# Two output-gate blocks moved from the attention's filler into the gate stage, and the second value tiles computed in another order

## The chip, the cores and the metric

The kernel runs on one core of one Trainium2 chip. The metric is the device time of one execution in microseconds; lower is better. The program is one launch that reads float32 inputs from DRAM and writes a float32 output of 1024 x 1024.

## The reference

One streaming-encoder block on 16 meta tokens and 1024 tokens of width 1024. What matters here is the mixer:

```python
u = rmsnorm(h, norm_mix)
a, q, k, v, r, lr, ga, gb = split(u @ w_in)             # widths 512, 256, 256, 512, 512, 16, 1024, 1024
y_a = (mix(multiscale_pool(a)) * pool_scale) @ w_pool_out
o   = gla_chunked(q, k, v, log_sigmoid(lr @ w_gate_up + b_gate) / 16)     # 4 heads, chunks of 64 tokens
y_b = (rmsnorm(o, gla_norm) * silu(r)) @ w_gla_out
m   = sigmoid(ga) * y_a + sigmoid(gb) * y_b
h   = h + m @ w_out
```

A squared-ReLU feed-forward layer (1024 to 4096 to 1024) and a last norm follow. The change concerns 256 of the 1024 columns of `gb`, which are blocks 6 and 7 of 128 columns, and the order in which one half of `v` is computed.

## The kernel before

All large products run on TensorE as three products each: every operand is split into a high part (rounded by ScalarE, `act.activation(hi, raw, ACT.Copy)`) and a low part (the rest, by VectorE or GpSimd), and high times high, high times low and low times high are summed in PSUM (`mm3`, L245 to L251). A "product" below is one such matmul of 128 x 128 weights on 512 columns, unless another width is given. Tokens lie in two halves of 512; meta tokens stand ahead of half 0. The normed input sits in SBUF as `th` and `tl` (high and low, one pair for each half).

The stages follow each other:

1. **Start** (L690): norm, transposes, the first half of `v`.
2. **Gate stage** (`Quarters` L286, `gate_result` L891, `gate_stage` L932): blocks of 128 output columns of `w_in` are computed in pairs. For a pair and the two token halves, the 2 x 2 product over two halves of the inner dimension is formed from seven quarter products (P1 to P7) instead of eight. Each quarter product is 4 inner tiles of 128 x three matmuls of 512 columns, so a pair costs 7 x 12 = 84 products, where the plain way (`project`, L447) costs 2 blocks x 2 halves x 8 tiles x 3 = 96. `BLOCKS` (L616) lists 20 blocks, so ten pairs: `ga` 0 to 7, `q`, `r`, and `gb` 0 to 5. Results go to DRAM (`ga_dram`, `q_dram`, `r_dram`, `gb_dram`).
3. **Pooling** and the first block of `k`.
4. **Attention** (`gla`, L1524): four units (pair of heads, token half) in the order (0,0), (1,0), (0,1), (1,1). Of each unit, `inside` (decays and scores, L1359) runs beside `across` (states and output, L1445) of the unit before. These are chains of small steps that pass between engines, and TensorE would wait in them. So work called filler is poured between the steps: `fill` (L1276) is a list of independent projections, and after each step `pour` takes as many products from it as cover the latency that the step states in its `yield`. The order of TensorE's instructions is therefore written out when the program is built, and it is fixed. Filler, in order: second block of `k`; second half of `v` (`v_second`); the last two blocks of `gb` the plain way (`gb_pair(6)`); `y_a` (`ya_block`, 4 x 48 products); `y_b` of half 0 (`yb_block(j, 0)`, 4 x 24 products). What is left after the last unit runs behind it.
5. `y_b` of half 1, out projection, feed-forward, last norm. `early_gates` (L1202) fixes the recorded order on ScalarE and VectorE from the last `across` on.

Steps of the last `across` by line: L1402 and L1403 make the decayed keys `mix` (`kl`) and queries; L1456 transposes the keys on TensorE and L1457 copies them to SBUF; L1464 multiplies keys by values into PSUM tile `b_m` (bank `m2`, of which there is one, L1126); seven steps at L1470 run the state from chunk to chunk on VectorE; L1479 and L1489 make the output in the same bank, with a one-column read by ScalarE between them (L1484); L1498 squares, L1501 sums, L224 to L233 take the inverse root, L1503 scales, L1507 transposes, L1514 and L1516 multiply by the silu gate, L1518 rounds to `yg` and L1521 takes the low part. `y_b` of half 1 reads that `yg`.

Steps of one output of the filler: `ya_block` multiplies by the gate at L1058 (VectorE) and stores to `ma_dram`; `yb_block` of half 0 multiplies by the `gb` gate at L1257 and adds `ma` at L1262 (both VectorE), stores the sum (ScalarE's DMA queue, L1265), rounds it at L1268 (ScalarE) and takes the low part in two pieces at L1272 (GpSimd).

`pooled_back` (L1147) loads the pooled operand (four DMAs of 1 MB, GpSimd's queue) over `th` and `tl` of half 1, once nothing else reads those; `ya_block` needs it. `gate_load` (L1036) loads one `ga` gate tile.

## Time and profile before

| | us |
|---|---|
| median of 3 runs | 1192.87 (1192.79 to 1193.24) |
| the profiled execution | 1193.63 |
| its span, first to last instruction | 1191.9 |
| gate stage, steady part | about 43 to 237 |
| pooling, first `k` | about 237 to 302 |
| attention with filler | about 302 to 463 |
| `y_b` of half 1, out projection, feed-forward | about 463 to 1184 |
| VectorE, ScalarE busy | 895.5 (75%), 643.5 (54%) |
| DMA mean rate | 167 GB/s |

Stage borders are read from the times at which the lines of each stage run in the trace. Times of rows below are microseconds from the start of the span. A matmul's busy time overlaps the next one, so its price is the distance between starts. Waits are put down to what ended last.

### The profile page before, as it was taken

What the parts mean: (1) busy time and instruction counts of PE and PEld (TensorE: products, weight loads), DVE (VectorE), ACT (ScalarE), POOL (GpSimd) and SP (SyncE); (2) the same over time, 40 slices, a digit from 0 to 9 for tenths busy, and PEclk for the clock granted to TensorE, in tenths of its full rate; (3) what the DMA queues carried; (4) which work ended last, traced back from release to release, by engine and by line L of the source; (5) the groups of instructions that cost most, each with busy time, mean ns of one, the idle gap of its engine ahead of it and who ended that gap; (6) DMA issues with size and microseconds to landing.
All of it is one profiled execution on the core that took longest, in us unless ns stands there. A gap on an engine that the chain in (4) does not pass through costs nothing.

```text
span 1191.9 us, 18477 instructions
## 1 busy us (share of the span) xinstructions
PE 1177.9 (99%) x6762; PEld 985.7 (83%) x6762; DVE 895.5 (75%) x1436; ACT 643.5 (54%) x1172; POOL 76.1 (6%) x122
## 2 busy tenths in 40 slices
PE   8999999999999999999999999999999999999997
PEld 8888888898998887788888888888888888888885
DVE  7886577657667887998996677767665887787695
ACT  7767567754546432548754554545554444445454
POOL 2200010000103226010000000000000000000000
PEclk9999999999999999999999999999999999999999
DMA  8247784435206677993264444445399963333532
GB/s 261 37 115 178 220 193 126 150 111 156 72 20 242 193 250 253 329 247 131 91 201 146 165 151 141 159 137 181 125 310 321 335 193 95 99 95 97 168 98 89
DMA packets 149515, 199.03 MB, mean 167 GB/s; under 512 B 10712, under 2 KB 81136, under 8 KB 148624
## 3 DMA queue, kind: packets, MB, share of 16 engines
q1 hardware_dynamic: 142992, 179.69, 47.3%
q0 software_dynamic: 5120, 15.80, 5.8%
q10 hardware_dynamic: 1312, 2.36, 0.5%
q8 instruction: 53, 0.87, 0.3%
q14 instruction: 38, 0.31, 0.1%
HBM read 138.04 MB, written 68.16 MB: 173 GB/s over the span
## 4 chain that ended last, share of the span: by engine, by line
PE 92%; DVE 3%; DMA 3%; ACT 1%; issue 1%; POOL 0%; SPq 0%; ACTq 0%; DVEq 0%
PE b_mm L249 10%; PE b_mm L251 10%; PE b_mm L250 10%; PE b_ms L250 10%; PE b_ms L249 10%; PE b_ms L251 10%; PE b_x L250 8%; PE b_x L249 8%; PE b_x L251 8%; PE b_sc L1356 1%; PE b_mx L249 1%; PE b_mx L251 1%; PE b_mx L250 1%; DMA t<-gb_dram 1%; PE b_ms L1848 1%
## 5 line engine op out<-in xcount | busy, mean ns | idle before, releaser
L249 PE MATMUL b_mm<-th,w1h 128*128 128x512 f32 (+1 forms) x308 | 115.4, 375 | 0.8 <-DVE acc L1952 0.5
L251 PE MATMUL b_mm<-th,w1l 128*128 128x512 f32 (+1 forms) x308 | 114.2, 371 | 0.0
L250 PE MATMUL b_mm<-tl,w1h 128*128 128x512 f32 (+1 forms) x308 | 114.1, 371 | 0.0
L250 PE MATMUL b_x<-tl,w1h 128*128 128x512 f32 (+1 forms) x264 | 100.1, 379 | 0.0
L249 PE MATMUL b_x<-th,w1h 128*128 128x512 f32 (+1 forms) x264 | 100.1, 379 | 0.0
L251 PE MATMUL b_x<-th,w1l 128*128 128x512 f32 (+1 forms) x264 | 99.7, 378 | 0.0
L267 ACT ACTIVATE w1h<-raw 128x512 fp32r<-128x512 f32 x98 | 60.7, 620 | 25.2 <-PE b_ms L250 12.7
L268 DVE TENSOR_TENSOR w1l<-raw,w1h 128x512 fp32r<-128x512 f32 x98 | 67.0, 684 | 8.6 <-ACT w1h L267 8.6
L267 ACT ACTIVATE w1h<-fs 128x512 fp32r<-128x512 f32 x78 | 48.8, 628 | 43.6 <-PE b_ms L250 26.3
L249 PEld LDWEIGHTS b_mm<-th,w1h 128*128 128x128 f32 x308 | 57.8, 188 | 11.7 <-issue 1.6
L251 PEld LDWEIGHTS b_mm<-th,w1l 128*128 128x128 f32 x308 | 57.8, 188 | 10.1
L250 PEld LDWEIGHTS b_mm<-tl,w1h 128*128 128x128 f32 x308 | 57.9, 188 | 9.6
L268 DVE TENSOR_TENSOR w1l<-fs,w1h 128x512 fp32r<-128x512 f32 x78 | 53.3, 685 | 14.0 <-ACT w1h L267 13.8
L267 ACT ACTIVATE w1h<-bt 128x512 fp32r<-128x512 f32 x44 | 27.8, 632 | 66.6 <-issue 62.2
L251 PEld LDWEIGHTS b_x<-th,w1l 128*128 128x128 f32 x264 | 49.7, 188 | 9.5
L249 PEld LDWEIGHTS b_x<-th,w1h 128*128 128x128 f32 x264 | 49.6, 188 | 9.5
L250 PEld LDWEIGHTS b_x<-tl,w1h 128*128 128x128 f32 x264 | 49.6, 188 | 9.3
L2020 DVE TENSOR_TENSOR bt<-w,w 128x512 f32<-128x512 f32 x80 | 54.6, 683 | 0.0
L267 ACT ACTIVATE fxh<-bt 128x512 fp32r<-128x512 f32 x36 | 22.8, 632 | 56.3 <-issue 50.7
L1955 ACT ACTIVATE acc<-acc 128x512 f32<-128x512 f32 x48 | 30.3, 631 | 37.8 <-DVE acc L1952 37.8
L268 DVE TENSOR_TENSOR w1l<-rawx,w1h 128x512 fp32r<-128x512 f32 x44 | 30.1, 686 | 23.2 <-ACT w1h L267 23.2
L268 DVE TENSOR_TENSOR w1l<-bt,w1h 128x512 fp32r<-128x512 f32 x44 | 30.4, 690 | 20.9 <-ACT w1h L267 20.9
(537 smaller groups left out, 3411.5 us busy)
## 6 DMA issues: line engine op xcount, KB each, us to landing
hf_dram<-acc SPq DMA_DIRECT2D x112, 256.0 KB, 2.1
raw<-hf_dram SPq DMA_DIRECT2D x112, 256.0 KB, 2.6
w<-in_w_ff_dram SPq DMA_DIRECT2D x64, 256.0 KB, 4.5
raw<-in_w_in_dram SPq DMA_DIRECT2D x22, 512.0 KB, 4.7
raw<-in_w_ff_dram SPq DMA_DIRECT2D x16, 512.0 KB, 4.2
rawx<-in_w_ff_dram SPq DMA_DIRECT2D x16, 512.0 KB, 4.2
wt_dram<-in_w_out_dram POOLq DMA_DIRECT2D x6, 1024.0 KB, 10.6
rawx<-in_w_in_dram SPq DMA_DIRECT2D x10, 512.0 KB, 4.3
```

What stands on the lines that cost most here:

```text
L249: pe.matmul(ps, ah, bh, start=first and i == 0, stop=False, skip_group_check=more)
L250: pe.matmul(ps, ah, bl, start=False, stop=False, skip_group_check=more)
L251: pe.matmul(ps, al, bh, start=False, stop=last and i == n - 1, skip_group_check=more)
L267: act.activation(hi, a, ACT.Copy)
L268: low = lambda: dve.tensor_tensor(lo, a, f32(hi), ALU.subtract)
L1356: pe.matmul(b[to, e, j], kk[r, s], qq[r, s], start=True, stop=True, tile_position=(e * CH, u * CH))
L1848: pe.transpose(b[j][:, i], u[:, (4 * j + i) * P : (4 * j + i + 1) * P], ident)
L1955: act.activation(h[w], h[w] if u is not None else b, ACT.Relu)
L2020: dve.tensor_tensor(bt, w, S["w2"][q[3:]][:, i], ALU.add if q[2] == "+" else ALU.subtract)
```

## The change

`BLOCKS` gets `gb` blocks 6 and 7, so the gate stage computes eleven pairs. `gb_pair` and its `gb_block` are gone, and the filler with them is 96 products shorter; that also takes two weight blocks out of the filler's weight ring. `v_second` computes the tiles of token half 1 first, then the meta tile, calls `pooled_back` and `gate_load` twice (as `gb_pair` did), then the tiles of half 0. Lines behind `gb_block` stand 21 lower in the new file (L1262 is L1241), those behind the list of filler 22 lower (L1456 is L1434).

```diff
-        + [("r", h, C_R + h * P) for h in range(HEADS)] + [("gb", d, C_GB + d * P) for d in range(6)]
+        + [("r", h, C_R + h * P) for h in range(HEADS)] + [("gb", d, C_GB + d * P) for d in range(8)]
...
     def v_second():
-        for t in range(9):
+        for t in (4, 5, 6, 7, 8, 0, 1, 2, 3):
             rows, leave = v_tile(1, t, by_k=True)
             for k in range(0, KT, 2):
                 rows(k, 2)
                 yield 6 * 256 / 2400
             leave()
+            if t == 8:
+                pooled_back()
+                gate_load()
+                gate_load()
...
-    def gb_pair(d):
-        def fn(*wbs):
-            for half, at, n in MAIN[::-1]:
-                for u in range(2):
-                    yield from gb_block(d + u, [(half, at, n)], False)(wbs[u])
-                    if u and half:
-                        pooled_back()
-                    elif not half:
-                        yield "one"
-            gate_load()
-            gate_load()
-        return fn
...
-    step(fill, gb_pair(6), W1, [w_cols(C_GB + d * P) for d in (6, 7)])
```

**TensorE, the last `across`.** Before, between the output's first part (L1479) and its second (L1489), half 0 of `y_b` (`yg` is its operand, L249 to L251):

```order
L1479 MATMUL b_m_4729<-v_2711,scc 64x128 x16
L249 MATMUL b_mx<-yg_3510,w1h 128x512
L250 MATMUL b_mx<-yg_3510,w1h 128x512
L251 MATMUL b_mx<-yg_3510,w1l 128x512
L249 MATMUL b_mx<-yg_3510,w1h 128x512
L250 MATMUL b_mx<-yg_3510,w1h 128x512
L251 MATMUL b_mx<-yg_3510,w1l 128x512
L1489 MATMUL b_m_4729<-W,mix 64x128 x4
L1489 MATMUL b_m_4729<-S,mix 64x128 x2
L1489 MATMUL b_m_4729<-W,mix 64x128 x10
```

In the whole last `across`, 12 products of `y_b` stand ahead of the key transposes, 9 behind them, then 21, 6, 30 and 18 in the places that follow. Now (the first row is the last product of `y_b` of half 0, the last row is the first of half 1):

```order
L251 MATMUL b_mx<-yg_3655,w1l 128x512
L1434 MATMUL b_ms<-ident,mix 128x128 x4
L1442 MATMUL b_m_4808<-v_2850,mix 64x128 x16
L1457 MATMUL b_m_4832<-v_2850,scc 64x128 x16
L1467 MATMUL b_m_4832<-W,mix 64x128 x4
L1467 MATMUL b_m_4832<-S,mix 64x128 x2
L1467 MATMUL b_m_4832<-W,mix 64x128 x10
L1485 MATMUL b_m_4877<-ident,mix 128x128 x8
L249 MATMUL b_mm<-yg_3651,w1h 128x512
```

The filler ends ahead of the last `across`, and its six steps follow each other with nothing between them. Up to that place the number of products between two attention steps is the same in both programs; only their kind differs, `y_a` standing where `gb` stood and `y_b` of half 0 where `y_a` stood.

**VectorE, `inside` of the last unit beside `across` of the one before**, up to the sum of squares (TENSOR_REDUCE). Before, with the gate product of `y_a` (L1058) between the attention's steps:

```order
L1389 TENSOR_TENSOR n_2868<-n_2864,ends 128x16x2x16
L1391 TENSOR_TENSOR f<-n_2864,ends 128x16x32
L1419 COPY_PREDICATED scc<-mask,b_sc 128x512
L1058 TENSOR_TENSOR o<-b_mm,t_2715 128x512
L1419 COPY_PREDICATED scc<-mask,b_sc 128x512
L1389 TENSOR_TENSOR kq_2255<-n_2868,ends 128x8x2x32
L1391 TENSOR_TENSOR f<-n_2868,ends 128x8x64
L1058 TENSOR_TENSOR o<-b_mm,t_2715 128x512
L1501 TENSOR_REDUCE small<-mix 128x8
```

Now, with the two steps of a `y_b` output (L1236 is L1257, L1241 is L1262):

```order
L1367 TENSOR_TENSOR n_3007<-n_3003,ends 128x16x2x16
L1369 TENSOR_TENSOR f<-n_3003,ends 128x16x32
L1397 COPY_PREDICATED scc<-mask,b_sc 128x512
L1236 TENSOR_TENSOR t_2854<-b_mm,t_2854 128x512
L1397 COPY_PREDICATED scc<-mask,b_sc 128x512
L1241 TENSOR_TENSOR t_2854<-t_2854,o 128x512
L1367 TENSOR_TENSOR kq_2394<-n_3007,ends 128x8x2x32
L1369 TENSOR_TENSOR f<-n_3007,ends 128x8x64
L1236 TENSOR_TENSOR t_2854<-b_mx,t_2854 128x512
L1241 TENSOR_TENSOR t_2854<-t_2854,o 128x512
L1479 TENSOR_REDUCE small<-mix 128x8
```

Each output of filler in this unit now has two VectorE steps where it had one.

## Prediction

> **What bounds the kernel now.** I read the page first, then TensorE's waits, then stretches of the three stages that the change touches.

> ```profile
> span 1191.9 us, 18477 instructions
> PE 1177.9 (99%) x6762; PEld 985.7 (83%) x6762; DVE 895.5 (75%) x1436; ACT 643.5 (54%) x1172; POOL 76.1 (6%) x122
> PE b_m L1489 <- ACT small L1484: 1.3, 1, 1.3
> PE b_mx L249 <- DVE t L1257: 0.2, 1, 0.2
> 100.00:200.00 100.00, 100.00 (x438) 82.06 (x437) 67.72 (x106) 63.16 (x112) 7.44 (x14) 1.00 0.72 182
> 331.50:336.50 5.00, 5.00 (x44) 5.00 (x43) 2.70 (x10) 4.68 (x12) 0.46 (x1) 1.00 0.01 3
> 402.00:438.00 36.00, 36.00 (x456) 29.78 (x453) 30.56 (x57) 14.17 (x24) 7.73 (x8) 1.00 0.71 223
> ```

> TensorE (PE) is busy for 99% of the span, and its list of waits is short: the two rows above are the only ones inside the attention. Busy time alone proves little for pipelined matmuls, but the distance between starts does: in 100 us of the gate stage (columns: length, then busy time and count of PE, weight load, VectorE, ScalarE, GpSimd, then clock, DMA share, GB/s) there are 438 products, 0.228 us each, with VectorE 68% and ScalarE 63% busy. In the attention (402 to 438) PE never stops either. So the program is bound by the number of TensorE products, as long as filler covers the attention's chains. That condition is what the change touches: 12 products fewer in all, but 84 more in a stage that has no gaps and 96 fewer in one that needs them as cover.

> **The change part by part.**

> *Gate stage.* One more pair is 84 products x 0.228 = **+19.2 us**. The other engines' shares above are per pair, so they stay below one; two more weight blocks and four stores per pair lie within a DMA share of 0.72. Nothing else is on the path.

> *Filler up to the last `across`.* Between any two attention steps stand as many products as before, so PE's clock time there is unchanged as long as no step comes late: **0** in itself.

> *Order of the value tiles.* The same 216 products of 256 columns. `pooled_back` now goes out behind the meta tile, and 96 products of the half-0 tiles stand between it and the first `y_a`; 44 of them take 5.0 us in the second window above, so they cover 11 us, the attention's steps apart.

> ```profile
> tl<-pm_dram POOLq DMA_DIRECT2D x2, 1024.0 KB, 8.7
> ```

> The first half of that operand must land by then: 8.7 us is hidden, the second half is wanted one output (12 products, 2.7 us) later. If the cover failed, it would cost the 1 or 2 us by which a load is later. I take **0**. GpSimd's two weight blocks for `gb` (four pieces each) leave its queue, and `pooled_back` stands behind one of them less, so nothing there is later.

> *The last `across`.* Here the cover is gone. Before, from the start of `y_b` (438.45) to the start of the second half-1 block (470.00) PE runs 31.5 us, 108 products among them. Now PE reaches the same place with no half-0 product left, and the chain runs bare. Its steps, one engine at a time:

> ```profile
> 437.12 0.69 DVE L1516 TENSOR_TENSOR mix<-b_m,mix 128x512 f32<-128x512 f32 x1 [2.23 <-PE b_m L1507]
> 437.85 1.29 ACT L1518 ACTIVATE yg<-mix 128x512 fp32r<-128x512 f32 x2 [0.28 <-DVE mix L1516]
> 438.45 0.40 PE L249 MATMUL b_mx<-yg,w1h 128*128 128x512 f32 x1
> 439.12 0.42 DVE L1402 TENSOR_TENSOR mix<-kq,ends 128x256 f32<-128x256 f32 x1
> 439.45 0.69 DVE L1521 TENSOR_TENSOR yg<-mix,yg 128x512 fp32r<-128x512 f32 x1
> 440.39 0.74 DVE L1419 COPY_PREDICATED scc<-mask,b_sc 128x512 f32<-128x512 uint8 x1
> 440.51 1.06 ACT L1601 ACTIVATE wx<-raw 128x1024 fp32r<-128x1024 f32 x1
> 441.21 0.60 PE L1456 MATMUL b_ms<-ident,mix 128*128 128x128 f32 x4
> 441.62 0.68 DVE L1257 TENSOR_TENSOR t<-b_mx,t 128x512 f32<-128x512 f32 x1
> 441.84 0.60 ACT L1457 ACTIVATE mix<-b_ms 128x512 f32<-128x512 f32 x1 [0.27 <-PE b_ms L1456]
> 442.33 0.69 DVE L1262 TENSOR_TENSOR t<-t,o 128x512 f32<-128x512 f32 x1
> 443.80 1.10 PE L1464 MATMUL b_m<-v,mix 64*64 64x128 f32 x32
> 444.97 0.35 DVE L1470 SCALAR_TENSOR_TENSOR W<-S,ends,b_m 128x128 f32<-128x128 f32 x1 [1.95 <-PE b_m L1464]
> 445.36 2.27 DVE L1470 SCALAR_TENSOR_TENSOR W<-W,ends,b_m 128x128 f32<-128x128 f32 x6
> 449.86 1.10 PE L1479 MATMUL b_m<-v,scc 64*64 64x128 f32 x32
> 453.66 0.15 ACT L1484 ACTIVATE small<-b_m 128x2 f32<-128x2 f32 x1
> 455.10 1.03 ACT L1498 ACTIVATE mix<-b_m 128x1024 f32<-128x1024 f32 x1 [1.28 <-PE b_m L1489]
> 456.15 1.22 DVE L1501 TENSOR_REDUCE small<-mix 128x8 f32<-128x1024 f32 x1 [3.47 <-ACT mix L1498]
> 458.87 1.22 DVE L1503 TENSOR_TENSOR mix<-b_m,small 128x1024 f32<-128x1024 f32 x1
> 462.30 1.03 PE L1507 MATMUL b_m<-ident,mix 128*128 128x128 f32 x8
> 470.00 0.39 PE L249 MATMUL b_x<-yg,w1h 128*128 128x512 f32 x1
> ```

> On the clock of before: keys ready at 439.54 (L1402); transposes to 440.1; the copy L1457 stands behind the rounding of `wx` (1.06) in ScalarE's order, so it starts between 440.7 and 442.2, I take 441.0, nearer the early end, as `wx` waits for nothing of this chain, and ends at 441.6; keys by values 1.10, to 442.75 (VectorE has done the mask and the last merge by 442.5, in the same row lengths); seven state steps 0.35 + 2.27 and gaps, 445.5; L1479 needs the one bank that they read, so it follows, 446.6; ScalarE's look 0.15 + 0.1, 446.85; L1489 is as long as L1479, 447.95; square 1.03 + 0.13, 449.1; sum 1.22, 450.35; root, from L1501's end (457.37) to L1503's start (458.87), 1.5, 451.85; scale 1.22, 453.1; transposes 1.03, 454.15. From there to the end of the first half-1 block is 3.2 us: in the unit before, L1516 starts 0.04 behind the transposes (437.08), the second L1518 ends at 439.14, one more L1521 (0.69) follows, and then two products. So that block ends at 457.4 in place of 470.0: **-12.6 us** (-12.9 to -11.7 by the place of the copy). As a check: 96 x 0.228 = 21.9 saved, 9.3 paid back as waiting, net of the 1.5 in the two rows of waits, which go.

> *Two VectorE steps for one beside the last `inside`.* VectorE is busy 30.56 of 36 us there.

> ```profile
> L1058 DVE TENSOR_TENSOR o<-b_mm,t 128x512 f32<-128x512 f32 x6 | 4.1, 680 | 0.4 <-PE b_mm L251 0.4
> L1058 DVE TENSOR_TENSOR o<-b_mx,t 128x512 f32<-128x512 f32 x3 | 2.1, 685 | 0.0
> L1262 DVE TENSOR_TENSOR t<-t,o 128x512 f32<-128x512 f32 x8 | 7.1, 893 | 0.5 <-DMA o<-ma_dram 0.2
> ```

> Nine gate products of 0.68 are there now; about two stay and seven outputs of `y_b` come, each 0.68 + 0.69 to 0.89. That is 9.6 to 11.0 more and 4.8 less, 4.8 to 6.2 on an engine with 5.4 of slack, of which 2.2 is one wait for PE (the row of L1516). If all slack serves, under 1 us is left over; if only the 2.2 does, 2.6 to 4. The masks that free the score bank and L1503 stand behind these steps in VectorE's queue, and PE waits for both. I take **+1.5**, bounds 0 and 3.5. A gain is excluded, since PE does not wait there today.

> *The clock behind idle time.*

> ```profile
> 1.05 4.00 PE L739 MATMUL b_x<-fs 128*128 128x128 f32 x17 [1.05 <-DVE metab L1320]
> 4.62 1.69 PE L739 MATMUL b_x<-fs 128*128 128x128 f32 x12
> 1183.54 0.39 PE L251 MATMUL b_ms<-fxh,fxl 128*128 128x512 f32 x1
> 1186.00:1191.80 5.80, 0.00 (x0) 0.00 (x0) 1.36 (x5) 1.31 (x2) 0.00 (x0) 0.50 0.51 190
> ```

> The granted clock falls to 0.50 about 2.1 us after the last product (1183.93). At the start products come every 0.21 us until about 4.9, then about every 0.11 to 0.12 (12 in 1.69, which holds the last one's own 0.39): some 3.9 us of work at half speed, half of it lost, 2.0 us. The bare chain has a gap of 5.1 us (L1489's end to L1507) and one of 2.7 (the state steps). One closing costs 2.0, two 3.5 (the second hits L1479, L1489 and L1507, 3.2 us of work, at half speed). I take one, **+2.0**, bounds 0 and 3.5.

> [...]

> *Sum.* +19.2 - 12.6 + 1.5 + 2.0 = +10.1 us on the span of 1191.9: 1202.0, and 1203.7 with the 1.7 that lie around it in the profiled execution (1193.63). The median of the runs is 0.8 below that execution, so **1203.0**.

> **Rivals.**

> *The clock holds.* PE still does about 1 us of work in every 3 or 4, and one wait of 1.3 us stands in the rows of before with the clock at 1.00. Then 19.2 - 12.6 + 1.5 = +8.1: 1201.0. Chance 0.31. The forecast itself: 0.50.

> *`y_b`'s transfers stall VectorE.* Its L1257 and L1262 wait for loads, and they now stand in one queue with the attention's masks; the row of L1262 shows 0.5 us of waits, 0.2 of it for a load. A load late by its whole landing time would put the sum beyond +14.6: over 1207.5. Chance 0.07.

> *The chain is covered all the same, and the kernel gets faster.* This is the plain count: 12 products fewer, 12 x 0.228 = -2.7, 1190.2. It needs the last unit's bare waits to come to no more than the 1.5 that go today; the point from which the change is not slower is 4.2 us of waiting. For it: PE is the bound everywhere else. Against: the new order of TensorE has nothing between the six steps, and the square, sum, root and scale alone are 5.1 us. Chance 0.04. That waiting comes out between, so that the time is within 2.4 us of before: 0.03; between there and 1199: 0.05, both slower chains than PE, but with more of the work running ahead than I see.

> **How the numbers follow.** A measurement of this kernel can tell about 0.2% (2.4 us) from no change. The range takes the bounds: 19.2 - 12.9 = +6.3, so 1199.0 rounded down, to 19.2 - 11.7 + 3.5 + 3.5 = +14.5, 1207.5; it holds the forecast and the first rival, 0.81, and leaves out 0.19. Slower: 0.50 + 0.31 + 0.07 + 0.05 = 0.93; same 0.03; faster 0.04.

> **What would show it.** In the profile of the changed kernel, the gate stage should end 19 us later with no new wait. The list of TensorE's waits, nearly empty now, should show some 11 us in the last `across`: for the state steps (PE L1457 on DVE L1448), for the scale (PE L1485 on DVE L1481, about 5 us, the longest), for the key copy and for `yg`. The stretch from the last half-0 product to the second half-1 block should be near 19 us instead of 31.5, or 21 with a slow clock, whose row should show less than 1.00. If VectorE is crowded, PE's scores (L1334) and L1485 of the unit before wait 1 to 3 us. I am wrong if PE shows no waits there, if the gate stage grows by more or less than 19 us, or if loads of `ma` or `gb` end the longest waits.

## The result, and the profile after

The changed kernel takes **1209.97 us** (median of 4 runs, 1209.64 to 1211.26); the kernel before takes 1193.05 in the runs beside it. The ratio is 1.014 (95% interval 1.0128 to 1.0152): +16.9 us, slower as forecast, but beyond the range, which ended at 1207.5. The profiled execution took 1209.64, its span 1207.5, that is 15.6 us more than before, where the forecast's sum was +10.1.

From the page of the changed kernel:

```profile
PE 1181.2 (98%) x6750; PEld 989.4 (82%) x6750; DVE 905.2 (75%) x1452; ACT 646.9 (54%) x1178; POOL 69.3 (6%) x114
PEclk9999999999999997999999999999999999999999
```

One slice of the row of the clock is below 9: about 453 to 483 us. The list of what TensorE waited for (total, times, longest) now begins with the attention:

```profile
PE b_m L1485 <- DVE mix L1481: 6.1, 2, 5.2
PE b_ms L1434 <- ACT mix L1381: 3.8, 1, 3.8
PE b_m L1457 <- DVE W L1448: 2.9, 1, 2.9
PE b_sc L1334 <- DVE scc L1397: 2.0, 1, 2.0
...
PE b_m L1442 <- ACT mix L1435: 0.7, 1, 0.7
```

Five rows, six waits, 15.5 us, where before had 1.5. All lie in the last two units. In the last `across` the waits for the scale (5.2), for the states (2.9) and for the key copy (0.7) are those that were foretold; the 3.8 for the decayed keys was not. Beside the last `inside`, the 2.0 for the masks lies within the 1 to 3 that were foretold for a crowded VectorE, and the other wait of L1485 is 0.9.

The milestones follow, from the timeline of before (those that the prediction has not shown) and of the changed kernel (start, length, engine, line, tiles, and what ended the idle time ahead; `...` stands where rows of this selection are left out, and steps of other engines in between are not shown):

```profile
336.91 0.60 PE L1456 MATMUL b_ms<-ident,mix 128*128 128x128 f32 x4
...
436.05 1.03 PE L1507 MATMUL b_m<-ident,mix 128*128 128x128 f32 x8
```

```profile
355.83 0.60 PE L1434 MATMUL b_ms<-ident,mix 128*128 128x128 f32 x4
...
444.72 0.68 DVE L1367 TENSOR_TENSOR n<-n,ends 128x512 f32<-128x512 f32 x1
445.85 0.74 DVE L1369 TENSOR_TENSOR f<-n,ends 128x512 f32<-128x512 f32 x1 [0.45 <-ACT n L1368]
446.51 0.72 DVE L1397 COPY_PREDICATED scc<-mask,b_sc 128x512 f32<-128x512 uint8 x1
447.13 0.68 DVE L1236 TENSOR_TENSOR t<-b_mm,t 128x512 f32<-128x512 f32 x1
447.72 0.72 DVE L1397 COPY_PREDICATED scc<-mask,b_sc 128x512 f32<-128x512 uint8 x1
448.34 0.68 DVE L1241 TENSOR_TENSOR t<-t,o 128x512 f32<-128x512 f32 x1
448.93 1.22 DVE L1367 TENSOR_TENSOR kq<-n,ends 128x512 f32<-128x512 f32 x1
...
453.17 0.33 ACTq L1244 DMA_DIRECT2D plain_dram<-t  x1
453.54 1.03 ACT L1476 ACTIVATE mix<-b_m 128x1024 f32<-128x1024 f32 x1 [3.49 <-DVE t L1241]
459.83 1.06 PE L1485 MATMUL b_m<-ident,mix 128*128 128x128 f32 x8 [0.92 <-DVE mix L1481]
...
466.20 1.08 PE L1434 MATMUL b_ms<-ident,mix 128*128 128x128 f32 x4 [3.76 <-ACT mix L1381]
467.97 1.98 PE L1442 MATMUL b_m<-v,mix 64*64 64x128 f32 x32 [0.69 <-ACT mix L1435]
481.96 1.97 PE L1485 MATMUL b_m<-ident,mix 128*128 128x128 f32 x8 [5.19 <-DVE mix L1481]
487.82 0.40 PE L249 MATMUL b_x<-yg,w1h 128*128 128x512 f32 x1
...
1199.53 0.39 PE L251 MATMUL b_ms<-fxh,fxl 128*128 128x512 f32 x1
```

Four stretches between these starts hold the result. A: the attention's first key transposes. B: the last transposes of unit (0,1). C: the key transposes of unit (1,1), with which the bare chain begins. D: the second half-1 block (`b_x`). E: the last product.

| stretch, us | before | forecast | after | after less forecast |
|---|---|---|---|---|
| start to A | 336.91 | 356.1 | 355.83 | -0.3 |
| A to B | 99.14 | 100.6 | 104.00 | +3.4 |
| B to C | 5.16 | 3.5 | 6.37 | +2.9 |
| C to D | 28.79 | 19.85 | 21.62 | +1.8 |
| D to E | 713.54 | 713.5 | 711.71 | -1.8 |

(Forecast: A from 19.2; B with the 1.5 for crowding; C from the keys at 439.54; D from the chain's end at 457.4 and the 2.0 for the clock. Behind E the span is 0.4 shorter than before.) The last column sums to +6.0, less 0.4: the 5.6 us (5.5 with less rounding) by which the forecast of the span fell short. Between the medians it is 7.0 (1203.0 to 1209.97): the rest lies outside the span, and in the median, which the forecast took 0.8 below the profiled execution and which is 0.3 above it.

Three things are to be read from the rows. First, between 444.7 and 448.4 VectorE goes from step to step with one gap of 0.45: the masks (L1397) that TensorE waits for until 448.50 stand behind steps of the filler (L1236, and L1241 of the outputs ahead). Second, ScalarE's square (L1476) starts at 453.54, though its product had ended at 446.45; before, the same square started 0.07 us behind its product (427.59). Ahead of it in ScalarE's queue stands the store L1244 of a filler output, which waits for VectorE's sum L1241. Third, keys by values (L1442) take 1.98 instead of 1.10, and the last transposes 1.97 instead of 1.03: the granted clock is 0.50 there (the windows below).

The windows of the changed kernel show when the clock was granted (length, PE's busy time and count, granted clock, DMA share, GB/s); their borders lie on the grid that the edges of the clock's own record give:

```profile
445.62:449.03 3.41, 1.36 (x65) 1.00 0.89 305
449.03:452.45 3.42, 3.42 (x51) 0.50 0.56 145
...
462.69:466.10 3.41, 0.00 (x0) 1.00 0.52 193
466.10:469.51 3.41, 2.62 (x32) 0.50 0.91 255
469.51:472.93 3.42, 0.56 (x15) 0.50 0.56 206
472.93:476.34 3.41, 3.13 (x56) 0.50 0.02 5
476.34:479.75 3.41, 0.43 (x16) 1.00 0.00 0
479.75:483.17 3.42, 1.21 (x6) 0.50 0.00 0
483.17:486.58 3.41, 3.41 (x11) 0.50 0.00 0
```

All edges lie on one grid of 3.41 us. The clock reads 0.50 behind windows in which TensorE was busy for 1.36, 0.00 and 0.43 us, and 1.00 again behind windows with 3.42, 3.13 and 3.41. It closes three times, and six windows (20.5 us) run at half speed.

### The profile page after: what moved, and what is told of

Its sections match the earlier page's. It is cut to its first block, busy times and chain, and to the rows that moved or that the text cites. A ratio compares the mean times of both kernels' runs of the same rounds, so it can differ in the third digit from the quotient of the medians.

```text
span 1207.5 us, 18477 instructions
## 1 busy us (share of the span) xinstructions
PE 1181.2 (98%) x6750; PEld 989.4 (82%) x6750; DVE 905.2 (75%) x1452; ACT 646.9 (54%) x1178; POOL 69.3 (6%) x114
## 4 chain that ended last, share of the span: by engine, by line
PE 92%; DVE 5%; ACT 2%; issue 1%; DMA 0%; ACTq 0%; DVEq 0%
PE b_mm L249 10%; PE b_ms L250 10%; PE b_ms L251 10%; PE b_ms L249 10%; PE b_mm L251 10%; PE b_mm L250 10%; PE b_x L250 8%; PE b_x L249 8%; PE b_x L251 8%; PE b_sc L1334 1%; PE b_mx L249 1%; PE b_mx L251 1%; PE b_mx L250 1%; PE b_ms L1826 1%; DVE t L1241 0%
## 5 line engine op out<-in xcount | busy, mean ns | idle before, releaser
L249 PE MATMUL b_mm<-th,w1h 128*128 128x512 f32 (+1 forms) x292 | 108.8, 372 | 0.3 <-DVE c L900 0.3
L251 PE MATMUL b_mm<-th,w1l 128*128 128x512 f32 (+1 forms) x292 | 107.9, 369 | 0.0
L250 PE MATMUL b_mm<-tl,w1h 128*128 128x512 f32 (+1 forms) x292 | 107.8, 369 | 0.0
L250 PE MATMUL b_x<-tl,w1h 128*128 128x512 f32 (+1 forms) x272 | 103.3, 380 | 0.0
L249 PE MATMUL b_x<-th,w1h 128*128 128x512 f32 (+1 forms) x272 | 103.3, 380 | 0.0
L251 PE MATMUL b_x<-th,w1l 128*128 128x512 f32 (+1 forms) x272 | 102.9, 378 | 0.0
L249 PEld LDWEIGHTS b_mm<-th,w1h 128*128 128x128 f32 x292 | 54.8, 188 | 10.4 <-issue 1.0
L251 PEld LDWEIGHTS b_mm<-th,w1l 128*128 128x128 f32 x292 | 54.8, 188 | 9.3
L250 PEld LDWEIGHTS b_mm<-tl,w1h 128*128 128x128 f32 x292 | 54.8, 188 | 9.1
L251 PEld LDWEIGHTS b_x<-th,w1l 128*128 128x128 f32 x272 | 51.2, 188 | 9.8
L249 PEld LDWEIGHTS b_x<-th,w1h 128*128 128x128 f32 x272 | 51.1, 188 | 9.9
L268 DVE TENSOR_TENSOR w1l<-rawx,w1h 128x512 fp32r<-128x512 f32 x46 | 31.5, 688 | 26.5 <-ACT w1h L267 26.5
## 6 DMA issues: line engine op xcount, KB each, us to landing
wt_dram<-in_w_out_dram POOLq DMA_DIRECT2D x6, 1024.0 KB, 11.6
```

Of the source, the lines that this page charges most:

```text
L249: pe.matmul(ps, ah, bh, start=first and i == 0, stop=False, skip_group_check=more)
L250: pe.matmul(ps, ah, bl, start=False, stop=False, skip_group_check=more)
L251: pe.matmul(ps, al, bh, start=False, stop=last and i == n - 1, skip_group_check=more)
L268: low = lambda: dve.tensor_tensor(lo, a, f32(hi), ALU.subtract)
```

## The experiments

The main theory after the result: **the filler's output steps** (two on VectorE, a store and a rounding on ScalarE, low parts on GpSimd for each half-0 output) stand ahead of the chain in the engines' queues and make it late, and **the clock** closes in the gaps; each costs some microseconds and they add. The rivals: the gate stage or the value order costs more than forecast; it is the bare chain alone, at a slow clock; the waits are for transfers.

### The parts of the change by themselves

The kernel before, with the pair in the gate stage as well as in the filler:

```diff
-    ... [("gb", d, C_GB + d * P) for d in range(6)]
+    ... [("gb", d, C_GB + d * P) for d in range(8)]
```

> The kernel before, with the eleventh pair (gb 6 and 7) added to the gate stage; the filler's own pair stays, so those two blocks are computed twice. Theory A (the gate stage's term was right: 84 products x 0.228 us, nothing else): +19.2 us, 1211 to 1213 us, TensorE's waits in the attention as before. Rival B (part of the missing 6.8 us lies in the gate stage, in later loads or stores): 1215 us or more, and new waits before the attention.

Measured: 1213.83 us (ratio 1.0176, 1.0161 to 1.0192). In its trace the first key transposes start at 356.18, 19.27 later than before, and no new wait stands ahead of the attention: theory A for the gate stage, and B falls. The median is 0.8 above theory A's range. In the profiled execution, the slowest of the four, the stretches A to B and B to C are those of before, and all that it has beyond the 19.27 lies in the last `across` and behind it, where a wait that before has too was longer (3.6 for 1.3), and the clock closed behind it (474.07 to 480.90; the mean granted clock of this execution is 0.996, of before beside it 0.998 to 0.999):

```profile
PE b_m L1489 <- ACT small L1484: 3.6, 1, 3.6
```

The kernel before, with the order of the value tiles alone:

```diff
-        for t in range(9):
+        for t in (4, 5, 6, 7, 8, 0, 1, 2, 3):
```

> The kernel before, with only the order of the second value tiles changed (tiles 4 to 7, meta, 0 to 3); the pooled operand's load stays where it was. Theory A (the order is free): 1193 us, within 1.2 us of before. Rival B (the order puts a value tile or the meta tile where the first units' chain wants it, or changes loads): 2 us or more away, with new waits in the first 60 us of the attention.

Measured: 1192.74, ratio 0.9997 (0.9988 to 1.0007). The order is free.

### The filler's steps, and the clock

One VectorE step less for each output of half 0:

```diff
-                dve.tensor_tensor(to, gl, ml, ALU.add)
+                if h:
+                    dve.tensor_tensor(to, gl, ml, ALU.add)
```

> The changed kernel, with the eight sums of the half-0 output blocks left out (the ma tile is loaded and not added), so VectorE has one step for each output of the filler instead of two. Theory A (VectorE is over full beside the last inside; that alone makes TensorE wait 2.0 us for the masks, closes the clock there and makes the last unit's keys late): the 2.0 us wait and the first stretch at half clock go, the keys come 2 us sooner; 5 to 7 us less, 1203 to 1205 us. Rival B (the time is that of the bare chain and its slow clock alone): under 1.5 us less. Rival C (the waits are for transfers of gb or ma): the waits for the masks stay.

Measured: 1207.33, 2.6 less. The wait for the masks falls from 2.0 to 0.9, A to B to 101.63 from 104.00, and the first closing is gone. But B to C stays at 6.1, and the clock is then at half speed from 465.00 to 485.48 without a break: keys by values take 1.99 at 465.22, the last transposes 1.97 at 479.50, and the products behind them start 0.43 us apart until 485.10 and 0.23 apart from 485.51. The mean granted clock stays 0.990. The time lies between theory A and rival B: the crowding is there, and part of what it gives back is lost again (C to D is 22.3 instead of 21.6). Rival C falls, since the wait for the masks more than halved with the loads left in.

Products of no use in the gaps of the last `across`:

```diff
+        spare, yg = bank("mm"), S["yg"][0]
+
+        def warm(n):
+            for i in range(n):
+                pe.matmul(spare, yg[:, 0, 0, :P], yg[:, 0, 1], start=True, stop=True)
...
+        warm(5)
         b = quad(bank("ms"))
...
+        warm(3)
         for j in range(4):
...
+        warm(10)
         o = two("m2").rearrange("p e (j c) -> p e j c", j=4)
...
+        warm(20)
         b = two("m2").rearrange("p e (j c) -> p (e j) c", j=4)
```

> The changed kernel, with 38 products of no use (on an operand that is long there, into a bank that nobody reads) placed in the gaps of the last across: 5 ahead of the key transposes, 3 ahead of keys by values, 10 ahead of the output, 20 ahead of the last transposes. They fill waits and delay nothing if the gaps are what they seem. Theory A (the clock closes because TensorE does little in a window of about 3.4 us, and the slow products of the last across cost 4 to 4.5 us): the clock stays at 1.00 from 453 us on, keys by values take 1.10 us again instead of 1.99, 4 to 4.5 us less, 1205.5 to 1206 us. Rival B (those products are slow for another reason, or the chain is not on TensorE at all): within 1 us of the changed kernel, 1209 to 1211 us.

Measured: 1207.02, 2.95 less where theory A had 4 to 4.5; C to D is 18.86 instead of 21.62. The clock still closed once there, behind the 2.6 us that stayed open ahead of the key transposes (466.61 to 470.02): keys by values at 467.88 take 1.99, and from 470.00 to 484.90 the granted clock is 1.00. That goes with most of the missing microsecond: C to D is 17.94 in a run below in which the clock held.

GpSimd's low parts left out:

```diff
-                for c in halves_of_half[: 2 - 2 * h]:
+                for c in halves_of_half[:0]:
```

> The changed kernel, with the sixteen low parts that GpSimd takes of the half-0 outputs left out. VectorE's work is the same, but six of its steps with two operands from SBUF took 1.22 us instead of 0.68 between 429 and 453 us, while GpSimd was busy 60 to 78 per cent there. Theory A (beside GpSimd those steps are slow, and that is a good part of the crowding): they take 0.68 again where only L1251 ran, VectorE is 2 to 3 us less behind, the last transposes of the unit before come 1.5 to 3 us sooner; with the shorter hold of the three gate tiles 2 to 5 us less, 1205 to 1208 us. Rival B (the number of steps alone crowds VectorE): those steps stay at 1.2 us or the time within 1 us, 1209 to 1211 us.

Measured: 1208.9, 1.1 less; A to B 103.61. Theory A fails: all six steps of 1.2 us are still there. In the trace of the changed kernel each of them overlaps GpSimd's L88, the low parts of the weights (12 pieces between 428.7 and 452.6), and they stay when L1251 goes. What was gained lies elsewhere, and also beside GpSimd: a step of the unit before (L1499, at 463.54 in the changed kernel) takes 0.69 instead of 1.29, the decayed keys stand behind it in VectorE's queue, and B to C is 5.76 instead of 6.37.

Products of no use in every gap of the last two units (8 ahead of the scores that waited, 3 ahead of the transposes of the unit before, 11, 3, 10 and 20 in the last `across`), and then the same with light outputs, of which the sum, the rounding and the low parts are left out:

```diff
+            if (p, half) == (1, 1) and pair == (3, 4):
+                warmer("ms")(8)
...
+        if (p, half) == (0, 1):
+            warmer("ms")(3)
```

> The changed kernel with products of no use in every gap of the last two units: 8 ahead of the scores that waited 2.0 us, 3 ahead of the last transposes of the unit before, and 11, 3, 10, 20 in the last across. Theory A (two parts: the slow clock costs 2.2 to 2.6 us beside the last inside and 3.8 us in the last across; the rest is a late chain, which stays): the clock is 1.00 from 6 us to the end, 5.5 to 6.5 us less than the changed kernel, 1203.5 to 1204.5 us. Rival B (a clock held up only lets TensorE wait longer, since VectorE sets the pace): 1206 us or more.

Measured: 1207.82, which is rival B's range. Theory A fails beside the last `inside`: the clock stays up there (the mean of the execution is 0.997, where the changed kernel has 0.990), but A to B is 103.51, half a microsecond less than in the changed kernel, and B to C is longer (7.89). With the clock held up TensorE only waits longer there, and VectorE sets the pace. (The clock closed once, at 0.50 from 468.66 to 472.07.)

> As the run with products of no use in every gap, and of the half-0 outputs the sum, the rounding and the low parts are left out (the multiplication and the store stay), so VectorE has one step for each output, ScalarE and GpSimd none. Theory A (what is left beside the clock is these steps standing ahead of the chain's in the queues of VectorE and ScalarE): the scores and the last transposes of the unit before wait under 0.5 us, the keys come 2 us sooner, 3 to 4.5 us less than the run above, 1199 to 1201 us, which is what gate stage plus bare chain come to on their own. Rival B (the chain is long by itself, and the forecast's bare chain was too short): 1202 us or more.

Measured: 1202.55, 5.3 less than the run above, with a mean granted clock of 0.998, as in the kernel before; but beyond theory A's 1201, and in rival B's range. The trace shows why the number does not decide: the scores start at 448.38, as in the run above, and so directly behind the 8 products of no use (446.31 to 448.45). These held them up. So the two causes were taken apart without products there.

Light outputs alone, then with products of no use in the last `across` only (11, 3, 10, 20):

```diff
-                dve.tensor_tensor(to, gl, ml, ALU.add)
+                if h:
+                    dve.tensor_tensor(to, gl, ml, ALU.add)
...
-                act.activation(th, gl, ACT.Copy)
                 if h:
+                    act.activation(th, gl, ACT.Copy)
...
-                for c in halves_of_half[: 2 - 2 * h]:
+                for c in halves_of_half[:0]:
```

> The changed kernel, and of the half-0 outputs the sum, the rounding and the low parts are left out; no products of no use. Theory A (those steps make the scores, the last transposes of the unit before and the keys late): last transposes of the unit before 2.5 us sooner or more, keys under 4 us behind them instead of 6.4, no wait for the masks; what stays is the bare chain at a slow clock, about 3 us: 1202.5 to 1204.5 us. Rival B (the lateness has another cause, the loads or the chain itself): 1206 us or more.

> As the run above, with products of no use in the gaps of the last across alone (11, 3, 10, 20). Theory A (two causes that add): the clock is 1.00 through the last across, 2.5 to 3.5 us less than the run above, 1199.5 to 1201 us, which is the forecast without its terms for crowding and clock (19.2 - 12.6 = +6.6, 1199.5). Rival B (the bare chain is longer than forecast): 1202 us or more with the clock at 1.00.

Measured: 1205.67, which is 1.2 above theory A's range and below rival B's, and 1201.47 (ratio 1.0074, 1.0057 to 1.0091), half a microsecond above theory A's range and below rival B's. The waits and milestones of the light outputs:

```profile
456.59 1.07 PE L1486 MATMUL b_m<-ident,mix 128*128 128x128 f32 x8 [1.59 <-DVE mix L1482]
461.15 1.08 PE L1435 MATMUL b_ms<-ident,mix 128*128 128x128 f32 x4 [1.96 <-ACT mix L1382]
462.92 1.98 PE L1443 MATMUL b_m<-v,mix 64*64 64x128 f32 x32 [0.69 <-ACT mix L1436]
...
482.84 0.39 PE L249 MATMUL b_x<-yg,w1h 128*128 128x512 f32 x1
```

and with the clock held up as well:

```profile
455.92 1.06 PE L1500 MATMUL b_m<-ident,mix 128*128 128x128 f32 x8 [0.79 <-DVE mix L1495]
460.88 0.60 PE L1446 MATMUL b_ms<-ident,mix 128*128 128x128 f32 x4
462.66 1.10 PE L1455 MATMUL b_m<-v,mix 64*64 64x128 f32 x32 [0.48 <-ACT mix L1447]
...
478.82 0.40 PE L249 MATMUL b_x<-yg,w1h 128*128 128x512 f32 x1
```

The three steps that the light outputs leave out cost 4.3 us (1209.97 to 1205.67), the clock in the last `across` 4.2 (1205.67 to 1201.47); together 8.5. In the second trace the granted clock is 1.00 from 462 to 481, keys by values take 1.10 again, and C to D is 17.94, where the prediction's chain had 17.85. The rival of the bare chain alone falls, and so does the rival of transfers: the row of the sums (L1241) in the changed kernel has 0.1 us of idle time, that of the gate products (L1236) none, and no DMA stands in TensorE's list. What is left over the forecast lies in A to B (99.95, 0.8 over before) and B to C (4.96, where the forecast had 3.5).

The light outputs keep one multiplication and the store, and these still hold up ScalarE's square: it starts 4.5 us behind its product (446.31 to 450.83), where the changed kernel has 7.1 and the run without the sums 5.4. So 4.3 us is not the whole price of an output's steps; what the remaining two cost was not measured by itself.

### Giving the cover back

If 96 products of cover are missing, less can be poured where TensorE came late anyway. In the changed kernel it came to the output (L1457) of the first three units 4.2, 3.3 and 1.5 us after its operands were there.

```diff
-PACE, LEVEL = 1.1, 1.6
+PACE, LEVEL = 1.0, 1.6
```

> The changed kernel with every stated latency multiplied by 1.0 instead of 1.1, the rest as it is: 45 half-0 products then stand in the last across (15, 9, 21, 0, 0), and the gap ahead of the last transposes stays bare (5.2 us). Theory A: the cover counts, wherever it is taken from, so most of the loss goes, and what stays is the bare last gap with one closing of the clock, 5 to 8 us: 1195 to 1200 us. Rival B (waits move to the earlier units, which lose up to 2.3 us each): 1203 us or more.

```diff
-            yield len(pair) * LEVEL
+            yield 2.6 if pair == (1, 2) else len(pair) * LEVEL
...
+        end = (p, half) == (1, 1)
...
-        yield 4.4 if (p, half) == (1, 1) else 5.4
+        yield 3.4 if end else 4.2
...
-        yield 6.0
+        yield 4.6 if end else 5.0
```

(The two other latencies of `across` in front of the output, and the one behind ScalarE's look, are shortened in the last unit alone.)

> The changed kernel, with less filler poured where a step of the attention stood ready 1 to 4 us before TensorE came to it: the latency stated behind keys by values 5.4 to 4.2, behind the output 6.0 to 5.0, of the middle pair of scores 3.2 to 2.6, and in the last across 1.2, 1.0, 3.4, 0.6, 4.6. By the built order 51 half-0 products then stand between the last scores and the last transposes (15, 6, 18, 3, 9) instead of 3, and fewer beside the last inside. Theory A (the loss is a cover that was spent where it was not needed, and with it go the crowding of VectorE and the closings of the clock): the waits of the last across fall from 14 to 4 us or less, no or one closing, 1193 to 1197 us. Rival B (the slack was wanted: the earlier units now wait as much as the last one gains): 1206 us or more.

Measured: 1206.9 and 1204.28, 3.1 and 5.7 less than the changed kernel, and far from the 10 to 15 and 13 to 17 expected: theory A fails in its size. The first lies in its rival's range; the second, the spare cover, lies between its two. The cover moved, but the chain grew by nearly half of it: in the spare cover 48 more products (10.9 us) stand in the last `across`, and B to D is 32.95 instead of 27.99. Its timeline at the last square:

```profile
465.41 0.32 SPq L1169 DMA_DIRECT2D t<-gb_dram  x1
...
469.60 0.69 DVE L1236 TENSOR_TENSOR t<-b_mm,t 128x512 f32<-128x512 f32 x1 [6.14 <-PE b_mx L251]
470.33 0.69 DVE L1241 TENSOR_TENSOR t<-t,o 128x512 f32<-128x512 f32 x1
471.05 0.33 ACTq L1244 DMA_DIRECT2D plain_dram<-t  x1
471.42 0.63 ACT L1247 ACTIVATE th<-t 128x512 fp32r<-128x512 f32 x1 [5.35 <-DVE t L1241]
471.96 1.01 ACT L1477 ACTIVATE mix<-b_m 128x1024 f32<-128x1024 f32 x1
```

The output's product had ended at 467.23. The square (L1477) stands behind the store and the rounding of a filler output, these behind its two VectorE steps, and these most likely behind a gate tile, whose load goes out at 465.41 (4.1 us is the median of such loads there). Other borders (the edit is against the spare cover) let the square go first:

```diff
-            yield 2.6 if pair == (1, 2) else len(pair) * LEVEL
+            yield 2.6 if pair == (1, 2) and (p, half) != (1, 1) else 3.0 if pair == (1, 2) else len(pair) * LEVEL
...
-        yield 3.4 if end else 4.2
+        yield 2.8 if end else 4.2
```

> The spare cover with other borders: 3.0 instead of 2.6 for the middle scores of the last unit, 2.8 instead of 3.4 behind keys by values of the last across, so that no output of the filler ends just ahead of the last unit's square, and 12 products instead of 9 stand behind it. In the spare cover that square stood in ScalarE's queue behind the rounding of such an output, which waited for a gate tile issued at 465.4 us; it ran 4.7 us after its operand was there. Theory A (that order cost the 4.7 us): the square follows its operand by under 1 us, the wait before the last transposes falls from 7.5 to 2 to 4 us, 3 to 6 us less than the spare cover's 1204.3: 1198 to 1201 us. Rival B (the chain is late for VectorE all the same): within 1.5 us of 1204.3.

Measured: 1205.12, not better, as rival B had it. The square now follows at once, and the last wait falls to 2.2:

```profile
459.40 0.63 ACT L1247 ACTIVATE th<-t 128x512 fp32r<-128x512 f32 x1 [1.08 <-DVE t L1241]
459.94 0.58 ACT L1436 ACTIVATE mix<-b_ms 128x512 f32<-128x512 f32 x1
...
470.71 1.03 ACT L1477 ACTIVATE mix<-b_m 128x1024 f32<-128x1024 f32 x1 [1.81 <-PE b_m L1468]
```

But the same queue now holds up the key copy (L1436): it starts 2.05 us behind its transposes (457.89), behind a rounding that waits for VectorE. Where one place was mended, another step of the same outputs came first.

The first 12 products of `y_b` of half 1 (two outputs, inner tiles 0 and 1, finished in `yb_block`) ahead of the last transposes, with the spare cover and with the other borders:

```diff
+    step(fill, begin_half1)
```

> As the spare cover above, and the first 12 products of y_b of half 1 (two outputs, the two heads whose values come from the unit before) are taken ahead of the last transposes, so 21 products stand in the longest gap instead of 9. Theory A: that gap is covered to under 1 us, 2 to 3 us less than the spare cover alone, 1190 to 1195 us; near 1190.5, the plain count of 12 products fewer, if nothing else waits. Rival B (the gap before the last transposes was not on the path): within 1 us of the spare cover alone.

> The same borders, with the first 12 products of y_b of half 1 ahead of the last transposes as in the run before, and the turn of the banks mended, so that the outputs behind them use the same banks as without. Theory A (the 8 us that this cost before came from the banks' turn, which made the out projection wait 4.3 us, and not from the products): no new wait behind 540 us, the last gap filled with 24 products, 1.5 to 3 us less than the run with the borders alone, 1195 to 1199 us. Rival B (taking them early is itself harmful): more than the run with the borders alone.

Measured: 1212.9 and 1212.42, that is 8.6 and 7.3 more than without these products. The first run fails both its theory (1190 to 1195) and its rival. The second had the banks' turn mended, and its theory A fails too: the same wait is there in both, some 60 us behind the attention, in the out projection (L249 for `acc`, 4.3 us in the first of the two and 4.4 in the second), and the clock closes behind it (542.71 to 546.12 in the second, whose mean granted clock is 0.992 where the run with the borders alone has 0.994).

Why the out projection is later by that is not settled. No version found here beats the kernel before.

## Why the prediction was wrong

*Right.* The gate stage (19.2 forecast, 18.9 here, 19.3 when added alone); the order of the value tiles (0; ratio 0.9997); the pooled operand's load, for which nothing waits; the place of the loss; and the bare chain itself: 17.85 forecast from the key transposes to the second half-1 block, 17.94 measured once clock and output steps were out of the way.

*Luck.* The time lies where the prediction had put the rival of transfers (over 1207.5, chance 0.07), and not for that reason: none of TensorE's waits in the attention ends with a load.

*Crowding beside the last `inside`: 1.5 forecast, bounds 0 and 3.5, measured 4.9* (A to B, 104.00 against 99.14). This is the step that failed most: the count of slack. VectorE's free 5.4 us were set against 4.8 to 6.2 of added work, and ScalarE's queue stood in no term. The order of the steps on an engine is written out when the program is built. A sum that VectorE did late (L1241, 451.93 to 453.13) held up ScalarE's store (453.17), and that ScalarE's square, which came 7.1 us late (446.45 to 453.54); not all of it is the sum's, since 5.4 of the 7.1 stay when the sums are left out. The light outputs bring A to B down to 100.76, so at least 3.2 of the 4.9 are the outputs' steps; and the clock that closed there costs little by itself, since holding it up bought 0.5.

*Keys: 2.9 us that stood in no term.* "Keys ready at 439.54" took the first of two steps at L1402. The second follows 0.9 us later:

```profile
440.06 0.42 DVE L1402 TENSOR_TENSOR mix<-kq,ends 128x256 f32<-128x256 f32 x1
```

In the changed kernel the transposes start at 466.20, 0.1 us behind the second (466.10), and before at 441.21, well behind it: 0.9 us misread. The rest is again the filler's last outputs ahead of the chain: B to C falls from 6.37 to 4.56 with light outputs, and 0.6 of that to 5.76 with the low parts alone left out.

*The clock: 2.0 forecast, bounds 0 to 3.5, measured about 3.8* (C to D, 21.62 against the chain's 17.85). That the clock falls to 0.50 behind TensorE's gaps was right, the count wrong: three closings and not one, two of them in the last `across`. One closing at 2.0 was an estimate from the pace of the first products of before; that there would be one and not two was the author's choice, which no row of before shows. Holding it up there is worth 3.0 us in the changed kernel, 4.2 with light outputs.

*Paid back: 2.2 us.* Two waits of 0.5 us behind the attention, `w1l` at L88 and `acc` at L1952 in before's list, are not in the list after; the forecast kept all of before's time there. They make 1.0 of the 2.2; the rest is not settled.

So no single step put the time outside the range: crowding (4.9 against 3.5) and clock (3.8 against 3.5) both came out over the upper bounds that the end of the range (+14.5) holds together, and the late keys (2.9), which stood in no term, came on top; 2.2 was paid back. The rival "the clock holds" is refuted by the record of the clock (20.5 us at 0.50); the rival of a covered chain by 15.5 us of waits.

## What to carry to other kernels

Filler is not only TensorE time: each of its outputs brings steps for the other engines, and where these were queued ahead of the latency-bound chain here, the chain became longer by them (leaving out three of them gave 4.3 us back). So price filler by what it puts into the queues of VectorE and ScalarE, a store issued from a compute engine's queue included, and take as filler what has the lightest outputs. Before moving work out of a filler list, look where the list then ends: the last chain loses its cover first, and idle TensorE there was paid for twice in the changed kernel, once as waiting (8.8 us for the scale, the states and the key copy) and once as a slow clock (3.0 us for holding it up there, 4.2 with light outputs).

## What the runs showed of the hardware

```profile
469.38:472.80 3.42, 1.59 (x52) 1.00 0.50 188
472.80:476.21 3.41, 0.00 (x0) 0.50 0.20 77
```

```profile
445.07:448.49 3.42, 1.68 (x8) 1.00 0.76 216
448.49:451.90 3.41, 2.07 (x42) 1.00 0.83 282
```

Behind the window with 1.59 us of work the clock reads 0.50, behind the one with 1.68 it reads 1.00. The 2.0 us gap of the changed kernel (446.45 to 448.50) lies in one window, the one with 1.36, and 0.50 follows it. The 3.1 us gap of the run with the other borders, ahead of 449.83, lies on both sides of a border of the grid (448.49); its two windows hold 1.68 and 2.07, and the clock stays at 1.00. On the way back, 2.62 us of work left the clock of the changed kernel at 0.50 (466.10 to 469.51), and behind 3.13 it reads 1.00 (472.93 to 476.34). No run varied the work in a window by itself.

**VectorE beside GpSimd.** Steps of VectorE with two operands from SBUF (L1367, L1241 and L1369 at 433.67, 434.27 and 434.87 of the changed kernel, where GpSimd is idle) take 0.67 to 0.68 us. Six steps of these lines between 429 and 453 us take 1.20 to 1.22, and each ends 0.55 us after the end of a piece of GpSimd's L88 that was running when it began: the step at 448.93 (L1367, above) ends at 450.15, the piece ran from 448.34 to 449.61. The steps at 438.66 and 439.86 began beside such a piece too, which ended 0.13 and 0.07 us later, and took 0.68. Why these two did not become longer was not shown. The six stay when L1251, the same operation of GpSimd on other tiles, is left out. A later step of the changed kernel (L1499, at 463.54) ends at 464.83, 0.55 us after a piece of L1251 that ran from 463.56 to 464.27; without L1251 it takes 0.69. The first row is of the changed kernel, the second of the run without L1251:

```profile
463.54 1.29 DVE L1499 TENSOR_TENSOR yg<-mix,yg 128x512 fp32r<-128x512 f32 x1 [0.66 <-ACT yg L1496]
463.21 0.69 DVE L1499 TENSOR_TENSOR yg<-mix,yg 128x512 fp32r<-128x512 f32 x1 [0.65 <-ACT yg L1496]
```
